# FFN matmuls of a decoder block on one Trainium2 core: some K-tile pairs by seven block products instead of eight, in 1024-column blocks

## The chip, the cores and the metric

The kernel runs on one core of a Trainium2 chip. Times are microseconds (us) on the device, from the first to the last instruction and what lies around them; a version's time is the median of several runs. Busy times, waits and granted clocks come from one profiled execution, whose instruction trace is read through views: a page, groups of instructions, windows of time, a timeline, the chain of waits. TensorE (PE) multiplies matrices, VectorE (DVE) and ScalarE (ACT) work elementwise, SyncE (SP) issues the loads.

## The reference, cut to what matters

One layer of a decoder: attention and a gated recurrence side by side, merged and projected, then the FFN that the change is about. Batch 1, 256 positions, width 2048, FFN width 5632, all in float32.

```python
a = rmsnorm(h, norm_ffn_pre[layer])
gt, up = jnp.split(a @ w_ffn_gate_up[layer], [D_FF], axis=-1)
ff = (jax.nn.silu(gt) * up) @ w_ffn_down[layer]
h = h + rmsnorm(ff, norm_ffn_post[layer])
```

## The kernel before, in words

**Precision.** Every float32 operand of a matmul is split into a high part (ACT rounds it to the matmul's type, fp32r) and a low part (DVE subtracts the high part from the operand). A product is then three matmuls, high x high, high x low, low x high, accumulated in one PSUM bank.

**Tiles.** All matmuls against weights run from one list of blocks. A block is 512 output columns of one weight matrix over its whole K. Its work is cut into chunks of two K tiles (128 rows each) by 512 columns, 512 KB. In the FFN the activations are the stationary operand (128 x 128), the weights the moving one (128 x 512), and each chunk has 2 K tiles x 2 sides (positions 0 to 127, 128 to 255) x 3 = 12 matmuls into two PSUM banks, one a side. Gate and up are 11 blocks each, in turn, with K = 16 tiles; down is 4 blocks with K = 44 tiles.

**Order.** One loop runs over all chunks, and the program order on each engine is the order in which this loop issues. For chunk i it issues the split of chunk i+2 (`split`, L214 on ACT, L215 on DVE), the load of chunk i+8 (`load`, L196 on SP, six slots `raw`), the matmuls of chunk i (`multiply`, through `mm`, L90), and then one piece each of what waits in queues: `evacs` (what empties a block's banks), `turns` (transposes of results), `lanes` (attention and recurrence, long done in the FFN). Each engine works in its program order, so an instruction that waits holds all behind it. The split parts have three slots, so the split of chunk i+2 writes where chunk i-1 was read.

**FFN.** `evac_ffn_gate` takes a Sigmoid on ACT and a multiply on DVE (L964), `evac_ffn_up` multiplies by it (L973). The result is transposed on PE (L286, eight 128 x 128 transposes per 512 columns) and split once (L266, L267) into `act`, which stays until down has read it four times. `evac_down` takes the sum of squares (L1015) and the gain (L1018) from the banks. The last four chunks (HELD) are split early and multiplied side by side, so that side 0 is finished (`finish`: the norm, the residual, the stores) while side 1 is multiplied.

**PSUM.** Two pools of four banks of 512 columns, `acc` for the blocks and `aux` for all else. A pool hands its banks out in turn.

Of the kernel before, what the change touches and what calls it, by code (L numbers as in the profile page):

```python
# [13 lines left out]
F32 = mybir.dt.float32  # L14
# [22 lines left out]
N_RAW, N_SPLIT, AHEAD, HELD, WARM, BRIDGE = 6, 3, 2, 4, 8, 6  # L37


class Block:  # L40
# [7 lines left out]
    def __init__(self, kind, w, nk, col, xs, evac, parity=False, pre=None, mid=None, post=None):  # L48
# [6 lines left out]
        self.banks = None  # L55


@with_exitstack
def tile_hybrid_block(ctx: ExitStack, tc: tile.TileContext, t, out):
# [23 lines left out]
    def aux():  # L83
        return auxp.tile([P, 512], F32, tag="aux", name=nm("aux"))

# [72 lines left out]
    blocks, chunks = [], []  # L158
# [25 lines left out]
    def load(j):  # L184
        if j >= len(chunks):
            return
        b, c = chunks[j][:2]
        raw = stream.tile([P, 1024], F32, tag="raw", bufs=N_RAW, name=nm("raw"))
# [9 lines left out]

    def split(j, only=None):
        if j >= len(chunks):  # L200
            return
        raw = chunks[j][2]
        if chunks[j][3] is None:
            if j < len(chunks) - HELD:
                chunks[j][3:] = [
                    stream.tile([P, 1024], F32R, tag=s, bufs=N_SPLIT, name=nm(s))
                    for s in ("wh", "wl")
                ]
            else:
                chunks[j][3:] = [rslot(s) for s in ("wh", "wl")]  # L210
# [6 lines left out]
    def multiply(j, sides=(0, 1)):  # L217
        b, c = chunks[j][:2]
        wh, wl = (w.rearrange("p (k c) -> p k c", k=b.per) for w in chunks[j][3:])
        if b.banks is None:  # L220
            b.banks = [accp.tile([P, 512], F32, tag="acc", name=nm("acc")) for _ in range(2)]
        for s in sides:
            if s == 1 and c == 0 and b.mid:
                b.mid()
            for kk in range(b.per):
# [18 lines left out]
                mm(b.banks[s][:, :S], l, xh, False, last)  # L244

# [663 lines left out]
    def more_h(c):  # L909
# [6 lines left out]
        if c == 5:  # L916
            end_phase1()

# [20 lines left out]
    def gslot(s):  # L939
        return act_pool[0].tile([P, 1024], F32, tag="g", bufs=3, name=nm(s))  # L940

    act_t, gate_t = [], {}

    def aslot(s):
        if len(act_t) < 8:
            return rslot(s)
        return act_pool[0].tile([P, 1024], F32R, tag="a", bufs=14, name=nm(s))

    def evac_ffn_gate(j):
        def go(banks):  # L950
            g = gate_t[j] = gslot("g").rearrange("p (b c) -> p b c", b=2)
            src = banks
            if "r2" not in ready:
                for i in range(2):
                    nc.scalar.activation(g[:, i, :], banks[i], AF.Copy)
                    yield
                src = [g[:, i, :] for i in range(2)]
                while "r2" not in ready:
                    yield
            for i in range(2):  # L960
                s, r = ptile("sig"), r2c[:, i : i + 1]
                nc.scalar.activation(s, src[i], AF.Sigmoid, scale=r)
                yield
                nc.vector.scalar_tensor_tensor(  # L964
                    out=g[:, i, :], in0=src[i], scalar=r, in1=s, op0=OP.mult, op1=OP.mult
                )
        return go

    def evac_ffn_up(j):
        def go(banks):  # L970
            g = gate_t[j]
            for i in range(2):
                nc.vector.tensor_mul(g[:, i, :], banks[i], g[:, i, :])  # L973
                yield
            for i in range(2):
                act_t.append(Split("act", 2, aslot))
                turns.append(act_t[-1].turned(g[:, :, i * S : (i + 1) * S], 0, 1))
        return go

    def act(k):  # L980
        while k // 2 >= len(act_t):
            advance(evacs)
        while not act_t[k // 2].there:
            advance(turns)
        return act_t[k // 2](k % 2)


    fss, fz, fpost = [], {}, []

    def begin_down():  # L990
        nc.scalar.preload_act_table_set("natural_log_exp_and_others")
        fss.append(small("fss"))
        for j in range(2):
            fpost.append(gslot("fpost"))
# [5 lines left out]
    def evac_down(j):  # L1000
        def go(banks):
            for i in range(2):
                down_side(j, i, banks[i])
                yield
# [192 lines left out]
```

## Time and profile before

| | |
|---|---|
| median of 3 runs | 1767.65 us (1767.29 to 1771.04) |
| the profiled execution | 1768.69 us, span of its instructions 1766.9 us |
| granted TensorE clock, mean | 0.997 |
| HBM read | 322.40 MB, 184 GB/s over the span |
| matmuls and transposes on PE | 8544 |
| DVE instructions, ACT instructions | 1151, 1019 |
| weight loads in the FFN | 176 + 88 of 512 KB |

The page gives each engine's busy time as a share of the span. A matmul's listed duration (0.39 us for 512 columns) is its latency: matmuls overlap, and the pace is read from their starts. In a timeline row the first two numbers are the start and the duration, in brackets stands the idle time of the engine just before and what ended it. In a row of the windows view, the engines' busy times are followed by the granted clock, the DMA engines' share and GB/s.

### The profile page before, as it was taken

What the parts mean: (1) busy time and instruction counts of PE and PEld (TensorE: products, weight loads), DVE (VectorE), ACT (ScalarE), POOL (GpSimd) and SP (SyncE); (2) the same over time, 40 slices, a digit from 0 to 9 for tenths busy, and PEclk for the clock granted to TensorE, in tenths of its full rate; (3) what the DMA queues carried; (4) which work ended last, traced back from release to release, by engine and by line L of the source; (5) the groups of instructions that cost most, each with busy time, mean ns of one, the idle gap of its engine ahead of it and who ended that gap; (6) DMA issues with size and microseconds to landing.
All of it is one profiled execution on the core that took longest, in us unless ns stands there. A gap on an engine that the chain in (4) does not pass through costs nothing.

```text
span 1766.9 us, 21907 instructions
## 1 busy us (share of the span) xinstructions
PE 1752.7 (99%) x8544; PEld 1472.1 (83%) x8544; DVE 1028.5 (58%) x1151; ACT 805.6 (46%) x1019; POOL 74.0 (4%) x54
## 2 busy tenths in 40 slices
PE   9999999999999999999999999999999999999998
PEld 7888888888888888888888878888888888888886
DVE  6667648877547775544565575555555555544444
ACT  6545445444444444454444474444444444443443
POOL 0002404300000000000000000000000000000000
PEclk9999999999999999999999999999999999999999
DMA  8666454456555665566657656666666666656663
GB/s 291 197 186 189 139 166 154 143 170 183 163 153 178 189 188 163 156 182 197 191 185 236 214 156 200 190 189 188 187 189 189 191 190 190 214 191 194 194 194 121
DMA packets 201224, 325.93 MB, mean 184 GB/s; under 512 B 10096, under 2 KB 76832, under 8 KB 201120
## 3 DMA queue, kind: packets, MB, share of 16 engines
q1 hardware_dynamic: 198848, 319.41, 59.2%
q10 hardware_dynamic: 2272, 5.12, 0.8%
q8 instruction: 67, 1.10, 0.3%
q14 instruction: 37, 0.30, 0.1%
HBM read 322.40 MB, written 2.10 MB: 184 GB/s over the span
## 4 chain that ended last, share of the span: by engine, by line
PE 98%; DVE 1%; ACT 0%; issue 0%; DMA 0%; POOL 0%; SPq 0%; DVEq 0%; ACTq 0%
PE acc L90 93%; PE aux L90 4%; PE aux L286 1%; PE aux L569 0%; PE aux L299 0%; DMA x<-in_x 0%; DVE x L621 0%; DVE fz L1039 0%; POOL x L615 0%; DVE b L607 0%; ACT wh L214 0%; PE aux L760 0%; SPq L196 0%; ACT junk L1015 0%; ACT junk L847 0%
## 5 line engine op out<-in xcount | busy, mean ns | idle before, releaser
L215 DVE TENSOR_TENSOR wl<-raw,wh 128x1024 fp32r<-128x1024 f32 (+1 forms) x601 | 748.0, 1246 | 704.0 <-ACT wh L214 700.6
L214 ACT ACTIVATE wh<-raw 128x1024 fp32r<-128x1024 f32 (+1 forms) x601 | 635.9, 1059 | 874.7 <-PE acc L90 865.3
L90 PE MATMUL acc<-wh,hT 128*128 128x512 f32 x1408 | 441.2, 391 | 0.3 <-ACT hT L306 0.3
L90 PE MATMUL acc<-wh,xT 128*128 128x512 f32 x1152 | 368.6, 395 | 0.0
L90 PE MATMUL acc<-xT,wh 128*128 128x512 f32 x1024 | 363.3, 400 | 0.0
L90 PEld LDWEIGHTS acc<-wh,hT 128*128 128x128 f32 x1408 | 264.3, 188 | 54.9 <-ACT hT L306 0.5
L90 PE MATMUL acc<-xT,wl 128*128 128x256 f32 x1024 | 287.0, 280 | 0.0
L90 PE MATMUL acc<-wl,hT 128*128 128x512 f32 x704 | 273.9, 389 | 0.0
L90 PEld LDWEIGHTS acc<-wh,xT 128*128 128x128 f32 x1152 | 219.0, 190 | 44.3
L90 PEld LDWEIGHTS acc<-xT,wh 128*128 128x128 f32 x1024 | 193.6, 189 | 46.3
L90 PE MATMUL acc<-wl,xT 128*128 128x512 f32 x576 | 225.4, 391 | 0.0
L90 PE MATMUL acc<-wh,act 128*128 128x512 f32 x704 | 217.6, 389 | 0.0
L90 PEld LDWEIGHTS acc<-xT,wl 128*128 128x128 f32 x1024 | 194.2, 190 | 0.1
L90 PEld LDWEIGHTS acc<-wh,act 128*128 128x128 f32 x704 | 132.1, 188 | 27.5
L90 PEld LDWEIGHTS acc<-wl,hT 128*128 128x128 f32 x704 | 132.3, 188 | 26.7
L90 PE MATMUL acc<-wl,act 128*128 128x512 f32 x352 | 136.9, 389 | 0.0
L90 PEld LDWEIGHTS acc<-wl,xT 128*128 128x128 f32 x576 | 109.5, 190 | 21.5 <-DVE wl L215 0.3
L90 PE MATMUL acc<-wh,yT 128*128 128x512 f32 x256 | 79.5, 390 | 0.0
L90 PEld LDWEIGHTS acc<-wl,act 128*128 128x128 f32 x352 | 66.1, 188 | 13.5
L90 PEld LDWEIGHTS acc<-wh,yT 128*128 128x128 f32 x256 | 48.1, 188 | 10.0
L90 PE MATMUL acc<-wl,yT 128*128 128x512 f32 x128 | 49.8, 389 | 0.0
L90 PE MATMUL acc<-wh,attnT 128*128 128x512 f32 x128 | 40.9, 391 | 0.0
(189 smaller groups left out, 989.8 us busy)
## 6 DMA issues: line engine op xcount, KB each, us to landing
raw<-in_w_in SPq DMA_DIRECT2D x271, 512.0 KB, 3.7
raw<-in_w_ffn_gate_up SPq DMA_DIRECT2D x176, 512.0 KB, 3.6
raw<-in_w_ffn_down SPq DMA_DIRECT2D x88, 512.0 KB, 4.5
raw<-in_w_mix_out SPq DMA_DIRECT2D x32, 512.0 KB, 3.8
raw<-in_w_attn_branch SPq DMA_DIRECT2D x16, 512.0 KB, 4.4
raw<-in_w_hgrn_branch SPq DMA_DIRECT2D x16, 512.0 KB, 4.0
hx<-in_x ACTq DMA_DIRECT2D x4, 512.0 KB, 10.0
x<-in_x SPq DMA_DIRECT2D x3, 512.0 KB, 9.5
```

Source lines behind the costliest of these rows:

```text
L90: nc.tensor.matmul(ps, lhsT, rhs, start=start, stop=stop, skip_group_check=True)
L214: nc.scalar.activation(wh[:, k], raw[:, k], AF.Copy)
L215: nc.vector.tensor_sub(wl[:, k], raw[:, k], wh[:, k].bitcast(F32))
L286: nc.tensor.transpose(ps[:, at : at + P], src[:, b, c : c + P], ident)
```

## The change

The FFN's columns are worked in blocks of 1024: a gate block and its up block together, or two down blocks. A step is two K tiles by 1024 columns, that is a 2 x 2 grid of weight tiles against a 2 x 2 grid of activation tiles (2 sides, 2 K tiles): eight block products of three matmuls each. For some K-tile pairs (`H7`: 3 of the 8 in gate/up; 6 of the 22 in down) the step is done by seven products, after Strassen: `split_wide` forms four sums of weight tiles on DVE, `seven_sums` four sums of activation tiles, three products go straight into the output banks, four into banks of their own (p1, p5, p6, p7), or the reverse share as `multiply_wide` lists it. At the last such step of a block `gather` combines the four extra banks in SBUF, and the evacuation adds that to the output banks. All eight PSUM banks are then in use by a block; the next one takes the pools the other way round. The first gate and up blocks stay as they were.

The sums for gate/up are made once (`h_sums`). For down the activations are kept in float32 (`turn_act`), and each of the two blocks splits them and forms their sums anew, step by step (`prep_act`). The gate takes Silu on ACT in one go. Loads, split parts and chunks of the earlier stages share slots twice as large and half as many. Instead of four held chunks, the last two steps are multiplied by side and column half.

Lines of the changed kernel: in `split_wide` L305/L306 (ordinary step: high part on ACT, low part on DVE), L310, L316, L317 (sums on DVE), L315, L318, L320 (high parts on ACT), L321, L322 (low parts on DVE); `gather` L367 to L371; `seven_sums` L379 to L385; transposes L1116, their copies L1117; `evac_ffn` L1150 (adds), L1153 (Silu), L1156 (multiply); the splits of down's activations L410, L411; `down_part` L1193 (add), L1195 (Square), L1198.

```diff
-N_RAW, N_SPLIT, AHEAD, HELD, WARM, BRIDGE = 6, 3, 2, 4, 8, 6
+H7 = (0, 1, 2)
+GATE_UP = [(3, 0), (4, 0), (0, 1), (5, 0), (1, 1), (6, 0), (2, 1), (7, 0)]
+DOWN = [(m, m in (2, 5, 8, 11, 14, 17)) for m in range(KF // 2)]
...
-            if j < len(chunks) - HELD:
-                chunks[j][3:] = [
-                    stream.tile([P, 1024], F32R, tag=s, bufs=N_SPLIT, name=nm(s))
-                    for s in ("wh", "wl")
-                ]
-            else:
-                chunks[j][3:] = [rslot(s) for s in ("wh", "wl")]
+            w = wslot()
+            chunks[j][3:] = [w[:, :1024], w[:, 1024:]]
...
+    def load_wide(n):
+        if n % 2 or n // 2 >= len(steps):
+            return
+        n //= 2
+        b, i = steps[n][:2]
+        m = b.order[i][0]
+        raw = stream.tile([P, 2048], F32, tag="raw", bufs=N_RAW // 2, name=nm("raw"))
+        for g, col in enumerate(b.cols):
+            src = b.w[2 * m * P : (2 * m + 2) * P, col : col + 512]
+            nc.sync.dma_start(
+                raw[:, g * 1024 : (g + 1) * 1024].rearrange("p (k c) -> p k c", k=2),
+                src.rearrange("(k p) c -> p k c", p=P),
+            )
+        steps[n][2] = raw
...
+        hi, lo = wslot(), p3("wl", F32R, 2048, 3)
+        if not by7:
+            nc.scalar.activation(hi, raw, AF.Copy)
+            nc.vector.tensor_sub(lo, raw, hi.bitcast(F32))
+            steps[n][3] = hi, lo
+            return
+        s, d = p3("sum", F32, 2048, 1), raw[:, 512:]
+        nc.vector.tensor_sub(
+            s[:, :1024].rearrange("p (a c) -> p a c", a=2),
+            raw[:, 512:1536].rearrange("p (a c) -> p a c", a=2),
+            raw[:, None, :512].to_broadcast([P, 2, 512]),
+        )
+        nc.scalar.activation(hi[:, :1024], s[:, :1024], AF.Copy)
+        nc.vector.tensor_add(s[:, 1024:1536], raw[:, 512:1024], s[:, 512:1024])
+        nc.vector.tensor_sub(s[:, 1536:], raw[:, 1536:], s[:, 1024:1536])
+        nc.scalar.activation(hi[:, 1024:], s[:, 1024:], AF.Copy)
+        dhi, dlo = p3("dh", F32R, 1536, 1), p3("dl", F32R, 1536, 1)
+        nc.scalar.activation(dhi, d, AF.Copy)
+        nc.vector.tensor_sub(lo, s, hi.bitcast(F32))
+        nc.vector.tensor_sub(dlo, d, dhi.bitcast(F32))
+        steps[n][3] = hi, lo, dhi, dlo
...
+        def prod(key, x, w, j, last=False):
+            ps = bank(key, 0 if type(key) is tuple else 1)
+            wh, wl = (v[:, j * 512 : (j + 1) * 512] for v in w)
+            mm(ps, x[0], wh, key not in b.open, False)
+            mm(ps, x[0], wl, False, False)
+            mm(ps, x[1], wh, False, last)
+            b.open.add(key)
...
+        if not by7:
+            for s in sides:
+                for g in groups:
+                    for k in range(2):
+                        prod((s, g), act_of(s, k), w, 2 * g + k, i == len(b.order) - 1 and k == 1)
+            return
+        t, d, sums = w[:2], w[2:], b.seven(m)
+        last = i == b.last7
+        prod((0, 1), act_of(0, 1), d, 2)
+        prod((0, 0), sums(3), d, 0)
+        prod("p1", act_of(0, 0), d, 1, last)
+        prod("p6", sums(1), t, 2, last)
+        prod("p5", sums(0), t, 1, last)
+        prod("p7", sums(2), t, 0, last)
+        prod((1, 1), act_of(1, 1), t, 3)
+    def gather(b):
+        e = {k: p3("e", F32, 512, 6) for k in ((0, 1), (1, 1), (0, 0), (1, 0))}
+        x = b.bank
+        nc.scalar.activation(e[0, 1], x["p1"], AF.Copy)
+        nc.vector.tensor_add(e[1, 1], x["p6"], e[0, 1])
+        nc.vector.tensor_add(e[0, 0], x["p5"], e[1, 1])
+        nc.vector.tensor_add(e[1, 0], x["p7"], e[0, 0])
+        nc.vector.tensor_add(e[1, 1], x["p7"], e[1, 1])
+        b.rest = e
+    def seven_sums(f, dst):
+        s = ptile("s").rearrange("p (n t) -> p n t", n=4)
+        a11, a12, a21, a22 = f[:, 0, :P], f[:, 1, :P], f[:, 0, P:], f[:, 1, P:]
+        for o, x, c, y in ((0, a21, -1.0, a22), (1, s[:, 0, :], -1.0, a11)):
+            nc.vector.scalar_tensor_tensor(
+                out=s[:, o, :], in0=x, scalar=c, in1=y, op0=OP.mult, op1=OP.subtract
+            )
+        nc.vector.tensor_sub(s[:, 2, :], a11, a21)
+        nc.vector.tensor_sub(s[:, 3, :], a12, s[:, 1, :])
+        nc.scalar.activation(dst[:, 0], s, AF.Copy)
+        nc.vector.tensor_sub(dst[:, 1], s, dst[:, 0].bitcast(F32))
...
+    def turn_act(u):
+        dst = aslot("act")
+        act_t.append(dst)
+        for i in range(2):
+            ps = aux() if wides.index(now[0]) % 2 else acc_bank()
+            for kk in range(2):
+                for s in range(2):
+                    at, c = kk * S + s * P, (2 * i + kk) * P
+                    nc.tensor.transpose(ps[:, at : at + P], u[s][:, c : c + P], ident)
+            nc.scalar.activation(
+                dst[:, 2 * i : 2 * i + 2, :], ps.rearrange("p (k t) -> p k t", k=2), AF.Copy
+            )
...
+    def evac_ffn(b):
+        e, x = b.rest, b.bank
+        for key in ((0, 0), (0, 1), (1, 0), (1, 1)):
+            nc.vector.tensor_add(e[key], x[key], e[key])
+            s, g = key
+            if g == 0:
+                nc.scalar.activation(e[key], e[key], AF.Silu, scale=r2c[:, s : s + 1])
+        yield
+        for s in range(2):
+            nc.vector.scalar_tensor_tensor(
+                out=e[s, 1], in0=e[s, 1], scalar=r2c[:, s : s + 1], in1=e[s, 0],
+                op0=OP.mult, op1=OP.mult,
+            )
+        turns.append([e[0, 1], e[1, 1]])
...
+    def prep_act(m, by7):
+        f = act_t[m // 2][:, m % 2 * 2 : m % 2 * 2 + 2, :]
+        x = parts_of[m] = Split("a", 2)
+        x.put(0, f)
+        if by7:
+            dst = rslot("so").rearrange("p (z n t) -> p z n t", z=2, n=4)
+            seven_sums(f, dst)
+            a7[m] = sums_of(dst)
...
+        nc.vector.tensor_add(f, b.bank[key], f)
+        sq, r2 = fss[0][:, 4 * i + j : 4 * i + j + 1], r2c[:, i : i + 1]
+        nc.scalar.activation(ptile("junk"), f, AF.Square, scale=r2, accum_out=sq)
...
+    def evac_down(b):
+        for i in range(2):
+            for j in range(2):
+                rest = down_part(j, i, b)
+                yield
+                rest()
...
+    w = t["w_ffn_gate_up"][0]
+    add("N", w, KD, 0, lambda k: hT[0](k), evac_first_gate,
+        pre=begin_ffn, mid=mid_ffn, post=more_h)
+    add("N", w, KD, FF, lambda k: hT[0](k), evac_first_up)
+    for j in range(1, 11):
+        add_wide_block(w, (512 * j, FF + 512 * j), GATE_UP, lambda k: hT[0](k),
+                       lambda m: h7[m], evac_ffn)
+    for j in range(2):
+        add_wide_block(t["w_ffn_down"][0], (1024 * j, 1024 * j + 512), DOWN, act,
+                       lambda m: a7[m], evac_down, prep=prep_act,
+                       pre=begin_down if j == 0 else None, turn=j == 0)
...
+        split_wide(i + AHEAD)
+        load_wide(2 * (i + AHEAD + N_RAW // 2))
+        if i >= len(steps) - 2:
+            break
+        multiply_wide(i)
+        if c == b.last7:
+            gather(b)
+        advance(evacs)
+        if c == 1 and b.turn:
+            flush(evacs)
+            turn_act(turns.popleft())
+        if c == len(b.order) - 1:
+            evacs.append(b.evac(b))
+            advance(evacs)
+    flush(evacs)
     for side in range(2):
-        for i in range(tail, len(chunks)):
-            multiply(i, (side,))
-        finish(side)
+        for g in range(2):
+            for i in (len(steps) - 2, len(steps) - 1):
+                multiply_wide(i, (side,), (g,))
+            finish(side, 2 + g)
 # ---- launch: one core; inputs and outputs as the reference has them ----
```

220 lines of the change are left out of this document (128 added, 92 removed).

## The prediction

> **What bounds the kernel now.** I read the page's busy line and its chain of work first, then the windows of the FFN, then the timeline of a few microseconds inside it.
>
> ```profile
> PE 1752.7 (99%) x8544; PEld 1472.1 (83%) x8544; DVE 1028.5 (58%) x1151; ACT 805.6 (46%) x1019; POOL 74.0 (4%) x54
> ...
> PE 98%; DVE 1%; ACT 0%; issue 0%; DMA 0%; POOL 0%; SPq 0%; DVEq 0%; ACTq 0%
> ```
> ```profile
> 1050.00:1500.00 450.00, 450.00 (x2025) 372.59 (x2024) 236.73 (x229) 196.40 (x210) 0.00 (x0) 1.00 0.65 190
> 1500.00:1750.00 250.00, 250.00 (x1109) 207.00 (x1107) 121.59 (x108) 103.80 (x108) 0.00 (x0) 1.00 0.59 189
> ```
>
> TensorE (PE) is busy for every microsecond of the FFN at granted clock 1.00, and the chain is 98% PE. VectorE (DVE) works 53% and 49% of these stretches, ScalarE (ACT) 44% and 42%. So a matmul taken away is time gained, as long as DVE and ACT keep ahead. The question is their order of work, so I need their paces:
>
> ```profile
> 1067.64 1.06 ACT L214 ACTIVATE wh<-raw 128x1024 fp32r<-128x1024 f32 x1 [1.66 <-PE acc L90]
> ...
> 1078.52 1.06 ACT L214 ACTIVATE wh<-raw 128x1024 fp32r<-128x1024 f32 x1 [1.66 <-PE acc L90]
> 1081.25 1.06 ACT L214 ACTIVATE wh<-raw 128x1024 fp32r<-128x1024 f32 x1 [1.66 <-PE acc L90]
> 1082.21 0.58 ACT L266 ACTIVATE act<-aux 128x512 fp32r<-128x512 f32 x1
> 1084.46 1.06 ACT L214 ACTIVATE wh<-raw 128x1024 fp32r<-128x1024 f32 x1 [1.66 <-PE acc L90]
> ```
> ```profile
> 963.34 0.69 DVE L860 TENSOR_TENSOR zg<-acc,gpost 128x512 f32<-128x512 f32 x1 [3.57 <-DMA gpost<-in_norm_mix_post]
> 963.95 1.22 DVE L215 TENSOR_TENSOR wl<-raw,wh 128x1024 fp32r<-128x1024 f32 x1
> ...
> 1058.00 0.75 DVE L964 SCALAR_TENSOR_TENSOR g<-acc,r2c,sig 128x512 f32<-128x512 f32 x1
> 1058.67 1.22 DVE L215 TENSOR_TENSOR wl<-raw,wh 128x1024 fp32r<-128x1024 f32 x1
> ...
> 1074.18 1.23 DVE L215 TENSOR_TENSOR wl<-raw,wh 128x1024 fp32r<-128x1024 f32 x1 [1.50 <-ACT wh L214]
> 1075.32 0.68 DVE L973 TENSOR_TENSOR g<-acc,g 128x512 f32<-128x512 f32 x1
> ...
> 1082.34 1.23 DVE L215 TENSOR_TENSOR wl<-raw,wh 128x1024 fp32r<-128x1024 f32 x1 [1.50 <-ACT wh L214]
> ```
> ```profile
> 604.90 0.69 DVE L528 TENSOR_TENSOR sum<-sum,tabs 128x512 f32<-128x512 f32 x1
> 605.63 0.69 DVE L529 TENSOR_TENSOR qk<-sum,w 128x512 f32<-128x512 f32 x1
> ```
> ```profile
> 1023.10 0.61 DVE L885 SCALAR_TENSOR_TENSOR h<-zg,rzc,hx 128x128 f32<-128x128 f32 x2
> 1023.63 0.20 DVE L102 TENSOR_SCALAR v<-zss,base 128x1 f32<-128x1 f32 x1
> ```
> ```profile
> 149.79 0.63 ACT L474 ACTIVATE sig<-q 128x512 f32<-128x512 f32 x1 [2.14 <-DVE q L473]
> ```
>
> PE: ACT's L214 is released by PE once a chunk; 1067.64 to 1078.52 is four chunks, 2.72 us each, and a chunk is 12 matmuls: **0.2267 us a matmul**. A chunk with four transposes takes 3.21 (1081.25 to 1084.46), so four cost 0.49. DVE starts the next instruction 0.60 us after one of 512 columns (963.34 to 963.95) and 1.14 after one of 1024 (1074.18 to 1075.32); by that line 2.22 after 2048 and 1.68 after 1536. A result is there 0.09 later, and an instruction that needs it starts 0.73 after the first (604.90, 605.63). A two-operation instruction of 512 takes 0.67, one of 128 0.27. ACT takes 1.06 for 1024 and 0.63 for 512, so 1.9 for 2048 and 1.5 for 1536, and starts 0.1 before it ends (1081.25, 1082.21). From ACT to DVE passes 0.04 (1082.31, 1082.34).
>
> **The change part by part.** *Removed:* three matmuls in each seven-product step. There are 3 in each of 10 gate/up blocks and 6 in each of 2 down blocks, 42 in all: 126 x 0.2267 = **28.6 us less**. An ordinary step now has 24 matmuls (5.44 us), a seven-product step 21 (4.76).
>
> *Added, gate/up* (line numbers of the changed kernel, as the section on the change gives them): DVE needs 2.22 for an ordinary step. In a seven-product step it makes the sums (1.27, 0.73, 0.73, each waiting for the last), waits for ACT's second rounding (1.06 + 0.04), then does the two low parts (2.22 + 1.68): 7.7 us, more than PE's 4.76. Over a block DVE has 3 x 7.7 + 5 x 2.22 + 2.66 (L368 to L371) + 2.40 (four adds, L1150) + 1.34 (L1156) = 40.6, PE 3 x 4.76 + 5 x 5.44 + 0.98 (transposes) = 42.5. It fits, but the order decides. Before a block ends (time 0), step 6 starts at -10.2; its start frees the weight slot, and from there ACT rounds (0.2 + 1.9), DVE does a low part (2.22), the gather (2.66), another low part (2.22) and the four adds (2.40): DVE is free at +1.45. Then comes the next block's first seven-product split (7.73), and only behind it L1156, whose result the transposes need: done at +10.6. PE has two ordinary steps, to +10.88. So the transposes are met with **0.3 us to spare**; the other two seven-product splits end 1.5 and 1.8 us before PE wants them. I take no loss here. This is the thinnest cover of the change: were it gone, PE waits in each of 10 blocks.
>
> The subtraction that reads one operand twice over (L310) is priced like a plain one, since the nearest row does just that:
>
> ```profile
> L522 DVE TENSOR_TENSOR w<-sum,tabs x48: 684/686/2415, 294.4 to 658.5; 64x512 f32<-64x512 f32 x48
> ```
>
> *Added, down:* each step first splits its own activations: 0.6 on ACT, 0.60 on DVE. A seven-product step also makes the activations' sums: two chained two-operation instructions, two subtractions, a wait for ACT (0.63), a low part: 2.45 more. So DVE needs 2.82 and 10.8 us, and for each three steps 10.8 + 5.64 = 16.4, where PE needs 4.76 + 10.88 = 15.64. DVE falls behind by 0.75 each time. Carried through both blocks: **8.6 us** of PE waits (five of 0.75 in the first block; 1.1, 1.4 and three of 0.75 in the second).
>
> At the start of down DVE holds L1156 behind the first seven-product step, which is now 3 us longer, and that step waits for ACT, which has a table load to do:
>
> ```profile
> 1516.17 1.28 ACT L991 ACT_TABLE_LOAD   x1
> ```
>
> ACT's last Silu ends at +2.2, the load at +3.4, the rounding at +4.0; DVE starts at +4.0, ends the step at +14.8, L1156 at +16.2. PE was ready at 10.88: **5.4 us**.
>
> Between the down blocks the four sums of the first are evacuated one per step (`evac_down`), each behind a split, and ACT's next rounding stands behind the Square of the last. One such round takes 0.8 (Square and the read of its sum, rows under *Tail*) + 0.6 + 1.9 + 2.22 + 0.67 + 0.6 = 6.8 us. The second block's first seven-product step needs the freed banks: the second at +13.1, the third at +19.9, the fourth at +26.7. PE reaches p5 at 14.6 and waits 5.3, then p7 and waits 6.1: **11.4 us**.
>
> *The clock.* Such gaps cost more than their length:
>
> ```profile
> 302.00:304.00 2.00, 0.70 (x6) 0.41 (x5) 2.00 (x3) 1.60 (x3) 2.00 (x2) 1.00 0.38 131
> 304.00:306.00 2.00, 2.00 (x16) 2.00 (x15) 2.00 (x1) 0.00 (x0) 1.35 (x1) 0.75 0.00 0
> 306.00:308.00 2.00, 2.00 (x8) 1.71 (x8) 2.00 (x4) 0.00 (x0) 0.00 (x0) 0.50 0.14 27
> 308.00:310.00 2.00, 2.00 (x12) 1.72 (x12) 1.44 (x3) 0.00 (x0) 0.00 (x0) 0.90 0.95 291
> ...
> 1762.00:1763.00 1.00, 0.00 (x0) 0.00 (x0) 0.96 (x3) 0.00 (x0) 0.00 (x0) 0.74 0.91 331
> ```
>
> After 1.3 idle us the clock (the column before the DMA share) is at half for 1.0 + 2.0 + 0.4 = 3.4 us, which loses 1.7; after the kernel's last matmul it halves near 1762.5. Three gaps of 5 to 6 us: 5.1 lost, of which I count 2.2 back, because a later PE waits less for the late splits: **2.9** (bounds 0 and 5.1). [...]
>
> *Tail:* the last side's banks are added to the gathered part (L1193) before the Square that today reads PSUM at once: 0.73 us more behind the last matmul.
>
> ```profile
> 1757.70 0.39 PE L90 MATMUL acc<-wh,act 128*128 128x512 f32 x1
> ```
> ```profile
> 1758.13 0.69 ACT L1015 ACTIVATE junk<-acc,r2c 128x512 f32<-128x512 f32 x1 [4.10 <-PE acc L90]
> 1758.71 0.19 ACT L1015 ACTIVATION_READ_ACCUMULATOR junk<-acc,r2c 128x1 f32 x1
> ```
>
> *Costed at nothing:* Silu in place of Sigmoid and a multiply (ACT has room in gate/up); the loads, now 1 MB a slot:
>
> ```profile
> raw<-in_w_ffn_gate_up SPq DMA_DIRECT2D x176, 512.0 KB, 3.6
> ```
>
> A slot is asked for about 7 us before it is read, two pieces of 3.6. In the stages ahead of the FFN every second load is released one chunk (2.72 us) later; they have five chunks in hand. If both covers fail, one to three us.
>
> **Sum:** -28.6 + 8.6 + 5.4 + 11.4 + 2.9 + 0.7 = **+0.4 us** on the profiled execution (1768.69; span 1766.9 and 1.8 around it). The median is 1.0 lower, so 1767.65 + 0.4 = **1768.0**. The step between engines is the softest duration: with 0 the waits shrink by 4, with 0.08 they grow by 5 (1 of it in gate/up). So 1763 to 1773 for this case.
>
> **Rivals.** *Faster:* the waits at the two seams of down (5.4 and 11.4, with 2.9 of clock) rest on the order in which DVE and ACT take their instructions and on which bank comes next. If banks come free earlier or the splits overlap better, only the lag stays: -28.6 + 8.6 + 0.7 = -19.3, 1748; with half of the seams, 1758. For it speaks that DVE has 47% of its time free today, against it that the instruction order of the changed kernel puts the adds behind the splits.
>
> *Slower:* the 0.3 us at the gate/up transposes. If DVE's run from the block's end to L1156 (some ten hand-overs) is longer by d, PE waits d - 0.3 in each of 10 blocks, and down lags more: d = 0.8 gives +5 there and +4 in down, 1777. It decides from d = 0.3 on. Against it: every duration in that run has its row. A variant: no DVE instruction starts before the last has ended, 0.09 more for each; the transposes are then 0.7 late and the down step 0.4 longer, +17 in all, 1785. The row 1075.32 speaks against it: it starts 0.09 before the one of 1074.18 ends. [...]
>
> *Not what it says:* fewer matmuls but a slower one, say by DVE's heavier traffic. In the windows above the pace is the same at 53% and 49% of DVE; a 1% slower matmul in the wide blocks would cost 6 us, 1774.
>
> **How the numbers follow.** Likeliest 0.40 (faster 0.05, within 0.28, slower 0.07); faster rival 0.28 (0.26 and 0.02 within); slower rival 0.25 (0.02 within, 0.23); not what it says 0.07 (0.02, 0.03, 0.02). With 0.2% (3.5 us, about what a measurement of this kernel can tell from no change): faster 0.33, within 0.35, slower 0.32. The range goes from half of the seams gone to just above d = 0.8: **1755 to 1779**, with about one in ten beyond each end.
>
> **What would show it.** Right: about 8420 matmuls at 0.227; in gate/up no PE wait above 0.3; in down PE waits of DVE of 5 to 6 us at three places, with the clock at half behind them, and some 0.7 before most seven-product steps; DVE over 75% busy in the FFN. Wrong: waits at L1116 in every block (the slower rival), or a PE without gaps in down (the faster one), or the matmul's pace off 0.227.

## The result, and the profile after

The changed kernel takes 1774.07 us (median of 9 runs, 1768.76 to 1774.66) where the kernel before takes 1768.37 (9 runs, 1767.29 to 1771.04): the ratio of their runs is **1.0023, 95% interval 1.0012 to 1.0033**, some 4 us slower by that ratio, while the medians lie 5.7 us apart. 1768.0 was forecast, within 1755 to 1779. Its profiled execution took 1772.15 us, with a span of 1770.4.

The page of the changed kernel, its busy line and its chain:

```profile
PE 1732.2 (98%) x8418; PEld 1451.0 (82%) x8418; DVE 1266.7 (72%) x1372; ACT 886.3 (50%) x1050; POOL 74.0 (4%) x54
...
PE 83%; DVE 11%; ACT 3%; issue 2%; DMA 0%; POOL 0%; SPq 0%; ACTq 0%; DVEq 0%
```

The 126 matmuls are gone (8544 to 8418). DVE is at 72% of the whole span, and it now stands for 11% of the chain: somewhere PE waits for it. The windows tell in which stage:

```profile
1050.00:1500.00 450.00, 448.84 (x2016) 371.04 (x2015) 387.65 (x331) 246.06 (x212) 0.00 (x0) 1.00 0.58 201
1500.00:1750.00 250.00, 232.57 (x1001) 188.96 (x1000) 204.66 (x216) 135.07 (x135) 0.00 (x0) 0.97 0.52 173
```

In gate/up PE idles 1.2 us in 450, in down 17.4 us in 250, at clock 0.97. The waits of PE from 1040 us on (total, times, longest):

```profile
PE aux L115 <- DVE e L1193: 10.4, 2, 5.3
PE acc L1116 <- DVE e L1156: 5.1, 2, 4.8
PE acc L115 <- DVE w L243: 1.2, 2, 0.8
PE acc L115 <- DVE dl L322: 1.0, 3, 0.5
PE aux L115 <- DVE dl L322: 0.8, 3, 0.3
```

The first two rows are the two seams of the forecast: the banks between the down blocks (L1193) and the multiply ahead of the transposes (L1156).

**A stretch that can be compared.** The profiles reach the FFN's second transpose between 1024.38 and 1030.07 us (more on this at the run of the kernel before, below), so I compare from that transpose on, to the start of the last matmul (the column FFN), and from there to the end of the span (the column tail). First the kernel before, then the changed one:

```profile
1024.87 0.59 PE L299 MATMUL aux<-ident,h 128*128 128x128 f32 x3 [0.75 <-DVE h L885]
```
```profile
1026.88 0.59 PE L443 MATMUL aux<-ident,h 128*128 128x128 f32 x3 [0.75 <-DVE h L1029]
...
1757.64 0.39 PE L115 MATMUL acc<-w,a 128*128 128x512 f32 x1
```

| us | FFN | tail | together |
|---|---|---|---|
| before | 732.83 | 9.20 | 742.03 |
| changed | 730.76 | 12.76 | 743.52 |

So of the 28.6 us of matmuls taken away, the FFN keeps 2.1, and the tail costs 3.6.

### The profile page after: what moved, and what is told of

The parts are those of the page before. It is cut to its first block, busy times and chain, and to the rows that moved or that the text cites. A ratio compares the mean times of both kernels' runs of the same rounds, so it can differ in the third digit from the quotient of the medians.

```text
span 1770.4 us, 21580 instructions
## 1 busy us (share of the span) xinstructions
PE 1732.2 (98%) x8418; PEld 1451.0 (82%) x8418; DVE 1266.7 (72%) x1372; ACT 886.3 (50%) x1050; POOL 74.0 (4%) x54
## 4 chain that ended last, share of the span: by engine, by line
PE 83%; DVE 11%; ACT 3%; issue 2%; DMA 0%; POOL 0%; SPq 0%; ACTq 0%; DVEq 0%
PE acc L115 65%; PE aux L115 16%; DVE wl L306 3%; DVE wl L321 1%; DVE dl L322 1%; DVE a L411 1%; DVE sum L310 1%; ACT w L305 1%; ACT w L318 1%; DVE w L243 0%; ACT w L242 0%; DVE w L666 0%; DVE sum L317 0%; DVE sum L316 0%; PE aux L443 0%
## 5 line engine op out<-in xcount | busy, mean ns | idle before, releaser
L243 DVE TENSOR_TENSOR w<-raw,w 128x1024 fp32r<-128x1024 f32 (+1 forms) x353 | 444.4, 1260 | 365.8 <-ACT w L242 363.7
L242 ACT ACTIVATE w<-raw 128x1024 fp32r<-128x1024 f32 (+1 forms) x353 | 373.0, 1057 | 481.4 <-PE acc L115 471.1
L115 PE MATMUL acc<-w,xT 128*128 128x512 f32 x1728 | 408.9, 395 | 0.0
L115 PEld LDWEIGHTS acc<-w,xT 128*128 128x128 f32 x1728 | 326.0, 191 | 65.8
L115 PE MATMUL acc<-xT,w 128*128 128x512 f32 (+1 forms) x2048 | 364.4, 339 | 0.0
L115 PEld LDWEIGHTS acc<-xT,w 128*128 128x128 f32 x2048 | 313.8, 189 | 46.1
L306 DVE TENSOR_TENSOR wl<-raw,w 128x2048 fp32r<-128x2048 f32 x82 | 187.5, 2287 | 28.0 <-ACT w L305 28.0
L305 ACT ACTIVATE w<-raw 128x2048 fp32r<-128x2048 f32 x82 | 156.5, 1908 | 67.9 <-PE aux L115 32.5
L115 PE MATMUL acc<-w,hT 128*128 128x512 f32 x622 | 182.5, 392 | 1.5 <-DVE w L243 1.2
L321 DVE TENSOR_TENSOR wl<-sum,w 128x2048 fp32r<-128x2048 f32 x42 | 96.3, 2293 | 47.3 <-ACT w L318 47.3
L315 ACT ACTIVATE w<-sum 128x1024 fp32r<-128x1024 f32 x42 | 44.6, 1062 | 96.3 <-DVE sum L310 92.0
L115 PE MATMUL acc<-wl,hT 128*128 128x512 f32 x215 | 83.6, 389 | 0.0
L322 DVE TENSOR_TENSOR dl<-raw,dh 128x1536 fp32r<-128x1536 f32 x42 | 73.6, 1752 | 0.0
L320 ACT ACTIVATE dh<-raw 128x1536 fp32r<-128x1536 f32 x42 | 61.9, 1473 | 0.0
```

Source lines behind the costliest of these rows:

```text
L115: nc.tensor.matmul(ps, lhsT, rhs, start=start, stop=stop, skip_group_check=True)
L242: nc.scalar.activation(wh[:, k], raw[:, k], AF.Copy)
L243: nc.vector.tensor_sub(wl[:, k], raw[:, k], wh[:, k].bitcast(F32))
L305: nc.scalar.activation(hi, raw, AF.Copy)
L306: nc.vector.tensor_sub(lo, raw, hi.bitcast(F32))
L315: nc.scalar.activation(hi[:, :1024], s[:, :1024], AF.Copy)
```

## The experiments

All but the repeat of the kernel before were made from the changed kernel. The times are medians, with the ratio to the kernel before on the same chip and its 95% interval. That kernel's medians beside them lie between 1768.98 and 1772.23, so times of different runs are compared by the ratio or by the stretches. FFN and tail are the stretches of the table, from one profile of each run; three profiles with the changed kernel's FFN lie within 0.5 us (730.32 to 730.76).

**Seven products in gate/up alone.**

```diff
-DOWN = [(m, m in (2, 5, 8, 11, 14, 17)) for m in range(KF // 2)]
+DOWN = [(m, False) for m in range(KF // 2)]
...
-        f = b.rest[key]
+        f = b.bank[key]
...
-        nc.vector.tensor_add(f, b.bank[key], f)
```

> Seven products in gate/up alone; all 44 down steps are ordinary ones, so there is no gathered part, the Square reads the bank and L1193 is gone. 90 matmuls less than before. Theory: 90 x 0.2267 = 20.4 us less, all kept but the 1.6 us of the first gate/up block: 1749 to 1750, no PE wait above 0.5 us behind the first block. Rival (the matmuls saved are paid in slower ones or in DVE's order in gate/up): 1760 or more.

Measured: 1755.09, ratio 0.9907 (0.9892 to 0.9922); FFN 714.13, 18.7 less than before where 20.4 - 1.6 = 18.8 was expected; tail 9.50. What PE waits for from the FFN's start on:

```profile
PE acc L115 <- DVE w L243: 1.2, 2, 0.8
PE aux L443 <- DVE h L1029: 0.8, 1, 0.8
PE acc L115 <- ACT hT L450: 0.3, 1, 0.3
```

The last two rows the changed kernel's first block has as well, and the kernel before has them too; only the first is the change's. The time was expected at 1749 to 1750 and is 5 more; the kernel before stood at 1772.23 in the runs beside it, 4 more than in the first ones, and this profile reached the FFN late (1030.07). By the stretch the gain of gate/up is kept, but for the first block.

**Seven products in down alone.**

```diff
-H7 = (0, 1, 2)
-GATE_UP = [(3, 0), (4, 0), (0, 1), (5, 0), (1, 1), (6, 0), (2, 1), (7, 0)]
+H7 = ()
+GATE_UP = [(3, 0), (4, 0), (0, 0), (5, 0), (1, 0), (6, 0), (2, 0), (7, 0)]
...
-            nc.vector.tensor_add(e[key], x[key], e[key])
```

The Silu and the multiply of `evac_ffn` then read the banks.

> Seven products in down alone; gate/up blocks are wide but all their steps ordinary, so nothing is gathered there. 36 matmuls less than before (8.2 us). Theory: the start of down costs 7, the seam between its blocks 14 (two bank waits and the clock), the lag 4, the tail 3.5: 28 to 29 lost against 8.2 gained, 1786 to 1790. Rival (down is not where the gain goes): 1768 or less.

Measured: 1786.99, ratio 1.0087 (1.0073 to 1.0101), 15.4 us slower by the ratio; FFN 744.87 (+12.0), tail 12.71 (+3.5). It is down that loses. The loss is some 5 us less than expected, 15.5 by the stretches where 28.5 - 8.2 = 20.3 was: the wait at the start of down is 2.0 instead of 4.8, since no adds of a gathered part stand ahead of the multiply there, and no half clock follows it. That the median still falls into 1786 to 1790 is luck: the kernel before was 4 us slower beside it.

**The order at the seams.** Three edits: the seven-product steps two later, the first down block evacuated at once, both.

```diff
-DOWN = [(m, m in (2, 5, 8, 11, 14, 17)) for m in range(KF // 2)]
+DOWN = [(m, m in (4, 7, 10, 13, 16, 19)) for m in range(KF // 2)]
```

> The changed kernel with one edit: the six seven-product steps of each down block are steps 4, 7, 10, 13, 16, 19 instead of 2, 5, 8, 11, 14, 17. The number of products is the same. Theory (order): at the start of down L1156 stands behind an ordinary split, so the 4.8 us wait for it and its clock drop (1.8) go; between the blocks the banks are free in time and one wait of about 4 us with a clock drop stays, because evacuation and splits still alternate: 15 us off the changed kernel, about 1759. Rival (DVE's total load in down is the bound): no change within 2 us, 1772 to 1776.

Measured: 1763.90, ratio 0.9960 (0.9948 to 0.9973); FFN 721.00, 9.8 less than the changed kernel, not 15. The wait for L1156 is gone. The seam between the blocks is not: PE waits 0.8, 2.1, 0.5 and 2.1 us there (L320 and L322, in the first two seven-product steps) and the clock drops twice (0.68 from 1650 to 1655 us, 0.66 from 1670 to 1675). Evacuation and splits still alternate, and the lateness lasts to the second of those steps, which I had not carried so far. And without the other seam every third step pays the lag, as PE's timeline of this run shows:

```profile
1543.04 0.50 PE L115 MATMUL aux<-dl,a 128*128 128x512 f32 x1 [0.28 <-DVE dl L322]
...
1559.24 0.50 PE L115 MATMUL aux<-dl,a 128*128 128x512 f32 x1 [0.27 <-DVE dl L322]
...
1575.46 0.50 PE L115 MATMUL aux<-dl,a 128*128 128x512 f32 x1 [0.28 <-DVE dl L322]
...
1591.67 0.50 PE L115 MATMUL aux<-dl,a 128*128 128x512 f32 x1 [0.28 <-DVE dl L322]
```

Three steps take 16.21 us (1591.67 - 1543.04 = 48.63 for nine): this is DVE's pace, since PE's own is 15.64 (the run with POOL's sums, below, has the same matmuls at that pitch). So the lag is 0.57 per seven-product step: the rival, DVE's total load, is right for this part of the loss.

The evacuation at once was tried first with an edit that had no effect: the condition picked blocks that never come to that line, and the order of instructions stayed that of the changed kernel.

```diff
-            advance(evacs)
+            if b.turn:
+                advance(evacs)
+            else:
+                flush(evacs)
```

> The changed kernel with one edit: at the end of the first down block all four sums are evacuated one behind the other, ahead of the next split, instead of one per step. Theory (order): the two bank waits of the second down block (5.3 and 5.2 us) go, but its first seven-product step (third step) is then split behind 5.4 us of evacuation: 5.4 + 10.8 = 16.2 against PE's 10.9, one wait of 5.3 at the low part of the differences in place of two, and one clock drop less: 6 to 7 us off the changed kernel, about 1767. Rival (DVE's total load in down is the bound, the order only moves the wait): no change within 2 us, 1772 to 1776.

Measured: 1774.39, ratio 1.0017 (1.0008 to 1.0026); FFN 730.32, tail 12.79. It tells nothing of the edit; it is a second profile of the changed kernel, and shows how well the stretches repeat. The mended edit:

```diff
-            advance(evacs)
+            if b is wides[-2]:
+                flush(evacs)
+            else:
+                advance(evacs)
```

> The changed kernel with one edit: at the end of the first down block its four sums are evacuated one behind the other ahead of the next split (this time the edit picks the first down block). Theory (order): the two bank waits of 5.3 and 5.2 go, one wait of about 5 us for the low part of the differences in the third step takes their place, and one of two clock drops goes: 6 to 7 us less between the FFN's second transpose and the last matmul (730.8 in the changed kernel). Rival (DVE's budget in down: what is not waited for at the seam is waited for in later steps): 3 us or less.

Measured: 1764.69, ratio 0.9973 (0.9963 to 0.9983); FFN 723.06, **7.7 less** than the changed kernel (6 to 7 expected). At the seam PE's timeline has now

```profile
1641.34 0.69 PE L115 MATMUL acc<-dh,a 128*128 128x512 f32 x1 [2.31 <-ACT dh L320]
1643.96 0.79 PE L115 MATMUL acc<-dl,a 128*128 128x512 f32 x1 [1.94 <-DVE dl L322]
```

4.2 us of waits for the split of the third step in place of 10.4 for the banks, as the order says, and the clock is at half for 6.8 us in place of 13.6. The lag does not take it back: the later waits for L322 stay at 0.3 us.

**The tail.**

```diff
-            nc.vector.scalar_tensor_tensor(
-                out=z, in0=z, scalar=r3, in1=h_t[j][:, i, lo:hi], op0=OP.mult, op1=OP.add
-            )
+            if i == 0 and j < 3:
+                nc.scalar.activation(z, z, AF.Copy, scale=r3)
+                nc.gpsimd.tensor_add(z, z, h_t[j][:, i, lo:hi])
+            else:
+                nc.vector.scalar_tensor_tensor(
+                    out=z, in0=z, scalar=r3, in1=h_t[j][:, i, lo:hi], op0=OP.mult, op1=OP.add
+                )
```

> The changed kernel with one edit in its tail: the first half's first three stores (scale and residual add, L1235) are done by ACT and POOL instead of DVE; the same values are computed. Theory (DVE's queue): in the changed kernel's trace the last matmul ends where it did before, and the end comes 3.5 us later, because the two adds L1193 stand behind 3.6 us of stores on DVE. Without the stores the add of the last bank follows its matmul at once: about 2.5 us off the changed kernel, 1771.5 where that has 1774.07. Rival (the chain is longer by its own add and waits, whatever DVE has queued): no change, 1774. The waits in down are not touched and stay at 5 us each.

Measured: 1775.83, ratio 1.0033 (1.0020 to 1.0046); tail 14.95, 2.2 *longer* where 2.5 less was expected. ACT's timeline:

```profile
1757.13 0.35 ACTq L1242 DMA_DIRECT2D out_dram<-fz  x1
1757.53 1.33 ACT L1236 ACTIVATE fz<-fz,r3c 128x512 f32<-128x512 f32 x2 [1.89 <-POOL fz L1237]
1760.84 0.35 ACTq L1242 DMA_DIRECT2D out_dram<-fz  x1
1761.23 0.72 ACT L1195 ACTIVATE junk<-e,r2c 128x512 f32<-128x512 f32 x1 [2.37 <-POOL fz L1237]
```

Two transfers are issued by ACT and wait for POOL's adds, and the Square waits behind them: the edit put a new wait in the place of the old one. The run with all edits, below, has SP issue these transfers.

**Tail and later steps together** (meant as all three edits, but with the evacuation edit that had no effect):

> The three edits together: stores of the first half on ACT and POOL in the tail, the first down block evacuated at once, and the seven-product steps of down at 4, 7, 10, 13, 16, 19. Theory (order): both seams close, the evacuation (5.4) and two ordinary splits (5.6) and the seven-product one (10.8) end at 21.8 where PE comes at 21.8; what stays of the 28.6 us lost is 1.6 in the first gate/up block, about 4 of lag in down and 1 in the tail: 22 us off the kernel before, 1746 to 1750, no PE wait above 1.5 us in down and the clock at 1.00 through down. Rival (DVE's total load in down is the bound): 1768 or more, the waits spread over many steps.

Measured: 1765.92, ratio 0.9973 (0.9963 to 0.9984); FFN 720.94 and tail 15.01. That is the FFN of the later steps alone (721.00) and the tail of the tail edit alone (14.95), and nothing else; the expected 1746 to 1750 needed the evacuation.

**DVE's budget.** On that version (its evacuation edit still without effect), the sums of activations on POOL:

```diff
+        if pool:
+            sub = nc.gpsimd.tensor_sub
+            sub(s[:, 2, :], a11, a21)
+            nc.gpsimd.tensor_add(s[:, 3, :], a21, a22)
+            sub(s[:, 1, :], s[:, 3, :], a11)
+            sub(s[:, 0, :], s[:, 2, :], a11)
+            sub(s[:, 0, :], s[:, 0, :], a22)
+            sub(s[:, 3, :], a12, s[:, 1, :])
```

> The version with all three edits (tail, evacuation at once, later seven-product steps), and the four sums of activations in each seven-product step of down are done by POOL instead of DVE (six subtractions and additions of 128 columns). Theory (lag by DVE's budget): DVE has 1.3 us less per three steps, 14.9 against PE's 15.64, and the lag goes: 2 to 4 us off the version with all three edits, 1744 to 1747. Rival (the lag is the wait for ACT's rounding, or POOL slows DVE): no gain, or slower.

Measured: 1759.28, ratio 0.9924 (0.9910 to 0.9937), where 1744 to 1747 was expected from a version at 1746 to 1750; FFN 713.35, 7.6 less than without (2 to 4 expected). The lag is gone: the matmul that waited for L322 every 16.21 us now starts every 15.64 (1521.33, then 1536.97, to 1599.53). The seam between the blocks is shorter too, with one clock drop instead of two (0.96 from 1630 to 1670 us, 1.00 from there to 1730), because the late splits are the same DVE work. From 1500 us on PE waits for

```profile
PE acc L115 <- DVE dl L322: 4.3, 2, 2.4
PE acc L115 <- DVE wl L306: 0.4, 1, 0.4
```

**The first gate/up block.** On that version, the sums for gate/up one block later:

```diff
-        if c == 6:
-            lanes[1].append(h_sums())
...
-    add("N", w, KD, FF, lambda k: hT[0](k), evac_first_up)
+    add("N", w, KD, FF, lambda k: hT[0](k), evac_first_up,
+        post=lambda c: lanes[1].append(h_sums()) if c == 1 else None)
```

> As the version with the sums on POOL, and the sums for the three activation pairs of gate/up are made one block later, over the second gate/up block instead of in the first, which also has the norm's sums. Theory: the 1.6 us of PE waits in the first gate/up block go: 1742 to 1746. Rival (these waits come from the loads): no change against the version with the sums on POOL.

Measured: 1759.72, ratio 0.9931 (0.9918 to 0.9943); FFN 715.72, 2.4 more. The waits for L243 in the first block are gone, so they did come from `h_sums` and not from the loads, but a wait of 1.9 us with a clock drop stands now at the first seven-product step, and at the seam of down the wait for L306 is 2.0 instead of 0.4. No gain, where 1742 to 1746 was expected.

**The cover in gate/up.**

```diff
+        nc.vector.scalar_tensor_tensor(
+            out=e[0, 1], in0=e[0, 1], scalar=1.0, in1=e[0, 1], op0=OP.mult, op1=OP.max
+        )
```

> The changed kernel with one DVE instruction of 512 columns more in each gate/up block, right ahead of L1156 (it takes a maximum of a tile with itself, so the values stay). In the changed kernel's trace L1156 ends some 0.2 us before the transposes that read it. Theory (the cover of the transposes is that thin): one more start-to-start time of 0.67 us leaves PE waiting 0.4 to 0.5 us in each of the 9 inner blocks and 0.7 more at the start of down: 4.5 to 5.5 us more between the FFN's second transpose and the last matmul (730.8 in the changed kernel), 1778. Rival (DVE is not in step with PE there, an earlier split makes up for it): 0.7 more, at the start of down alone.

Measured: 1778.77, ratio 1.0043 (1.0027 to 1.0059); FFN 736.84, **6.1 more** than the changed kernel (4.5 to 5.5 expected). In PE's timeline of this run

```profile
1345.45 0.27 PE L1116 MATMUL acc<-ident,e 128*128 128x128 f32 x1
1346.03 0.98 PE L1116 MATMUL acc<-ident,e 128*128 128x128 f32 x7 [0.31 <-DVE e L1159]
...
1388.35 0.27 PE L1116 MATMUL aux<-ident,e 128*128 128x128 f32 x1
1388.93 0.98 PE L1116 MATMUL aux<-ident,e 128*128 128x128 f32 x7 [0.31 <-DVE e L1159]
```

a block takes 42.90 us (1345.45 to 1388.35); in the changed kernel 42.41:

```profile
1342.51 1.03 PE L1116 MATMUL acc<-ident,e 128*128 128x128 f32 x8
...
1384.92 1.04 PE L1116 MATMUL aux<-ident,e 128*128 128x128 f32 x8
```

One instruction of 0.69 us (0.72 from its start to the next one's) costs 0.5 in each of nine blocks (4.4). The rest, 1.7, lies in down: the wait at its start is 0.7 longer (5.5 instead of 4.8), and more matmuls fall into the half clock behind the seams (behind the first, seven are listed with 0.63 us instead of 0.39; in the changed kernel two). The cover is as thin as the rows said.

**The kernel before again.**

> The kernel before once more, to see which part of a run's spread lies ahead of the FFN. The runs of all kernels reach the FFN's second transpose between 1024.4 and 1030.1 us by their profiles, the kernel before at 1024.87. If the spread belongs to the execution and not to the change, this profile comes to another start than 1024.87 within that range, with 732.8 from there to the last matmul and 9.2 behind it, both within 0.3.

Measured: FFN 732.86, tail 9.22, the FFN's second transpose at 1026.12. The stretches repeat within 0.03 us; the start does not. One thing that differs is the wait for the first load: 3.7 us in the run with gate/up alone (FFN reached at 1030.07), 1.1 in the run with all edits (1026.34):

```profile
PE aux L443 <- DMA x<-in_x: 3.7, 1, 3.7
```
```profile
PE aux L454 <- DMA x<-in_x: 1.1, 2, 1.0
```

The other is the clock. Over windows of 2 us up to 1024 us, time at half clock adds up to 3.4 us (a loss of 1.7) in the run with POOL's sums, which reached the FFN first (1024.38), to 6.8 in both profiles of the kernel before, and to 13.7 in the run with gate/up alone, which reached it last. Neither explains all: the run with the evacuation at once has a wait of 1.4 us and 6.8 us at half clock, and reached the FFN at 1028.47.

**All edits that helped:** later steps, evacuation at once, sums on POOL, and the tail with SP issuing the transfers.

```diff
+            eng = nc.sync if i == 0 else eng
             eng.dma_start(out[0, i * P : (i + 1) * P, j * 512 + lo : j * 512 + hi], z)
```

> The changed kernel with seven-product steps of down at 4, 7, 10, 13, 16, 19, the sums of activations on POOL, the first down block's sums evacuated at once ahead of the next split (this time the edit picks the right block), and the tail's first-half stores on ACT and POOL with their transfers issued by SP, so that ACT doesn't wait for POOL. Against the run with POOL's sums (729.3 us from the FFN's second transpose to the end, 14.97 of it behind the last matmul). Theory (order at the seam, DVE's budget in the blocks): the three waits of 2.4, 0.4 and 2.0 at the second block go, the tail falls to 10.5 to 11: 719 to 722 from the second transpose to the end, 1746 to 1749 in all, 1.2% under the kernel before. Rival (the evacuation only moves DVE's work, the lag appears elsewhere): 725 or more from the second transpose.

Measured: **1745.66, ratio 0.9864 (0.9849 to 0.9879)**, 1.4% faster than the kernel before; FFN 707.41 (25.4 less than before), tail 10.65, together 718.06 (719 to 722 expected). Of PE's waits the first gate/up block keeps its own (first row), and down has one left (second row):

```profile
PE acc L115 <- DVE w L243: 1.2, 2, 0.7
...
PE acc L115 <- DVE dl L322: 0.9, 1, 0.9
```

So 25.4 of the 28.6 us can be had in the FFN with the same products. What the changed kernel lost there went into the order of DVE's work at the seams and, as the lag shows, into its amount. This version changes both, since POOL takes the sums. The two order edits together without POOL were not run, so what order alone would give stays open.

## Why the prediction was right, and where not

The time was held by the range, and the likeliest case was the one that came: both seams cost what they were to cost, so the faster rival fell; PE's pace in a gate/up block is the forecast one, so the change does what it says; DVE is busy 86% of gate/up and 82% of down. But the sum came so close by luck, through errors of both signs, and the median lies 1 us above the 1763 to 1773 given for this case. Of the 6.1 us above 1768.0 the stretches from the FFN on explain 1.1. The forecast gave faster, within 0.2% and slower nearly equal chances, so that it came out slower is no success of it. Here a gap is the time from the start of the matmul ahead of it to the start of the one behind it, less 0.2267; it is about 0.16 longer than the wait that the row names.

| step | forecast | measured |
|---|---|---|
| matmuls removed | -28.6 | -28.6 |
| gate/up, inner blocks | 0 | 0 |
| first gate/up block | not priced | +1.9 |
| start of down | +5.4 | +5.5 |
| between the down blocks | +11.4 | +11.0 |
| lag in down | +8.6 | +2.8 |
| clock | +2.9 | +4.1 |
| tail | +0.7 | +3.6 |
| the rest (what is missing to the sum) | 0 | +1.2 |
| sum | +0.4 | +1.5 |

**Gate/up: right.** L1156 was to end 0.3 us ahead of the transposes. It ends 0.2 ahead: at 1172.53, with the transposes at 1172.74. The blocks' pitch is 42.4 (42.5 forecast). First DVE's row, then PE's:

```profile
1171.12 1.41 DVE L1156 SCALAR_TENSOR_TENSOR e<-e,r2c,e 128x512 f32<-128x512 f32 x2
...
1172.74 1.03 PE L1116 MATMUL acc<-ident,e 128*128 128x128 f32 x8
```

The slower rival was 0.2 us away in each block, and the run with one instruction more shows that it would have come.

**The seams: right, in place and size.** At the start of down L1156 comes behind the split, with PE's last matmul started at 1511.90 and DVE's late product ahead of it:

```profile
1512.38 2.29 DVE L321 TENSOR_TENSOR wl<-sum,w 128x2048 fp32r<-128x2048 f32 x1 [1.13 <-ACT w L318]
...
1514.59 1.75 DVE L322 TENSOR_TENSOR dl<-raw,dh 128x1536 fp32r<-128x1536 f32 x1
1516.26 1.41 DVE L1156 SCALAR_TENSOR_TENSOR e<-e,r2c,e 128x512 f32<-128x512 f32 x2
1517.06 0.33 PE L1116 MATMUL acc<-ident,e 128*128 128x128 f32 x1 [4.77 <-DVE e L1156]
```

Between the blocks each bank comes free with L1193, one round behind the other; 6.8 us were forecast for a round, and DVE's two L1193 and PE's two starts lie 6.82 apart:

```profile
1645.81 0.68 DVE L1193 TENSOR_TENSOR e<-aux,e 128x512 f32<-128x512 f32 x1
...
1646.55 0.80 PE L115 MATMUL aux<-w,so 128*128 128x512 f32 x1 [5.27 <-DVE e L1193]
...
1652.63 0.69 DVE L1193 TENSOR_TENSOR e<-aux,e 128x512 f32<-128x512 f32 x1
...
1653.37 0.80 PE L115 MATMUL aux<-w,so 128*128 128x512 f32 x1 [5.17 <-DVE e L1193]
```

**The lag: the size was off.** The step "DVE falls behind by 0.75 each time" was 0.57 (16.21 us per three steps, not 16.4), and it was charged ten times, while PE paid it six times (0.42 to 0.64 each): behind a seam DVE works on while PE stands, and the first steps of a block live on that lead. I added the lag to the seams as if they did not share a cause.

**The clock: too low.** I counted one drop of 3.4 us for each of three gaps and 2.2 of the 5.1 us back. There were two drops, of one and of four such stretches. The clock was at half from 1517.38 to 1520.80 and from 1643.68 to 1657.32 (rows in the last section); PE worked about 3.1 us of the first stretch and 5.2 of the second, and half of that, 1.5 + 2.6, is put down as lost: an estimate, since a matmul takes 0.43 us there from start to start (1654.39 to 1654.81) where it takes 0.2267 at full clock.

**The tail: the step "L1193 before the Square: 0.73 us more" failed.** I priced the added instruction, but not the queue on its engine. DVE's timeline:

```profile
1755.22 2.21 DVE L1235 SCALAR_TENSOR_TENSOR fz<-fz,r3c,h 128x128 f32<-128x128 f32 x4
1757.34 0.75 DVE L1198 SCALAR_TENSOR_TENSOR fz<-e,r2c,fpost 128x512 f32<-128x512 f32 x1
1758.12 0.75 DVE L1235 SCALAR_TENSOR_TENSOR fz<-fz,r3c,h 128x512 f32<-128x512 f32 x1
1758.79 0.68 DVE L1193 TENSOR_TENSOR e<-acc,e 128x512 f32<-128x512 f32 x1
...
1760.80 0.68 DVE L1193 TENSOR_TENSOR e<-acc,e 128x512 f32<-128x512 f32 x1
```

Before, ACT read the banks itself while DVE stored side 0. Now two adds stand behind these stores, and the last one starts 3.2 us after the start of the last matmul, with the Square behind it at 1761.52 (1758.13 before). In the run with all edits, where the stores are off DVE and ACT doesn't wait, it starts at 1734.82 with the last matmul at 1733.75, and the tail is 2.1 shorter.

**Not priced at all:** the sums of `h_sums` fall into the first gate/up block, where DVE and ACT also have the norm; PE waits 0.4 and 0.8 us for L243 there. I had counted them nowhere. The run with these sums one block later shows that they are the cause.

**What stays open.** The stretches from the FFN on differ by 1.5 us, the times by 4 (2 to 6 by the interval of the ratio; 5.7 by the medians). The rest lies ahead of the FFN, where profiles differ as much with the same code: the kernel before reaches it at 1024.87 and 1026.12, and the changed kernel and the runs made from it, with one code up to there, at 1024.38 to 1030.07. Whether the change's larger load slots add to that is not settled.

## What to carry to other kernels

Where an engine gets more work to take work off another one, price it at the seams of the loop, not at its mean: here DVE still had 18% of its time free in down (204.66 of 250 us busy), and 26.5 of 28.6 us were lost in the FFN, most of them where a long split stood ahead of a short instruction that PE waited for. An added instruction costs what its engine has queued ahead of it, here in the tail above all (3.6 us where 0.7 was priced). Once found, much of such losses goes by order alone: the long steps later gave 9.8 us, the evacuation ahead of the splits 7.7, each by itself. What the engine's amount of work costs in every round, here 0.57 us per seven-product step, stayed with the later steps and went where POOL took the sums.

## What the runs showed of the hardware

**In the stretches below the clock is at half for 3.41 us or a multiple of it.** Windows of 1 us in the changed kernel (the clock is the column before the DMA share):

```profile
1517.00:1518.00 1.00, 0.60 (x3) 0.42 (x4) 1.00 (x3) 0.00 (x0) 0.00 (x0) 0.69 0.34 94
...
1520.00:1521.00 1.00, 1.00 (x4) 0.77 (x4) 0.80 (x2) 1.00 (x3) 0.00 (x0) 0.60 0.85 330
...
1643.00:1644.00 1.00, 0.00 (x0) 0.00 (x0) 1.00 (x1) 0.00 (x0) 0.00 (x0) 0.84 0.06 23
...
1657.00:1658.00 1.00, 1.00 (x5) 0.84 (x4) 0.91 (x2) 0.06 (x1) 0.00 (x0) 0.84 0.00 0
```

In windows of 0.02 us around the four edges given next, the clock reads 1.00 or 0.50, but for the window that holds the edge. So 0.69 over 1 us is half clock for 0.62 us: it was at half from 1517.38 to 1520.80, 3.42 us, and from 1643.68 to 1657.32, 13.64 = 4 x 3.41. In the run with the evacuation at once (clock 0.75 from 1641 to 1642, 0.84 from 1648 to 1649) it was 1641.50 to 1648.32, 2 x 3.41. From 1517.38 to 1643.68 are 126.30 us, 37.0 times 3.41. Each of these half stretches follows one in which the windows view has PE busy for 0.3 to 1.5 of 3.41 us, and one with 1.73 us (1510.56 to 1513.97) was followed by full clock; around the two bank waits, 6.82 us apart, it was low over four of them. Busy time alone does not tell a half stretch from a full one: in the kernel before the clock was at half from 332.32 to 335.72 behind a stretch in which the view has PE busy throughout (3.41 us, 328.91 to 332.32), most of it with matmuls of 64 columns and of one column (32 of them from 327.80 to 331.37). In the run with the evacuation at once a wait of 2.3 us stands ahead of the first half stretch, and one of 1.9 us within it, ahead of the second. What sets the clock these runs do not show.

**With the sums on POOL some of the same DVE instructions took longer.** From 1525 to 1630 us, without POOL's sums (the run with tail and later steps) and with them:

```profile
L322 DVE TENSOR_TENSOR dl<-raw,dh 128x1536 fp32r<-128x1536 f32 x5 | 8.8, 1751 | 0.0
...
L316 DVE TENSOR_TENSOR sum<-raw,sum 128x512 f32<-128x512 f32 x5 | 3.5, 692 | 0.2
```
```profile
L322 DVE TENSOR_TENSOR dl<-raw,dh 128x1536 fp32r<-128x1536 f32 x5 | 9.5, 1908 | 0.0
...
L316 DVE TENSOR_TENSOR sum<-raw,sum 128x512 f32<-128x512 f32 x5 | 3.9, 778 | 0.2
```

That is 9% and 12% on the mean of five; single ones took 2.00 us (L322 at 1637.56) instead of 1.75 and 0.83 (L316 at 1632.50) instead of 0.69. L310 and L321 took no longer (1.21 and 2.30 us, 1.22 and 2.29 without). A subtraction of 128 columns took POOL 0.46 us as L383 and L384 of its run and 2.51 as L385, each the mean of nine (DVE itself 0.29); what sets POOL's time, and whether each of the longer DVE instructions ran beside POOL, these figures do not show. It still paid: DVE's idle time for ACT's rounding of the sums (L384 of the other run) was 3.5 us in this stretch without POOL, and none with it.
